# Score matmuls in turn on two row halves, and a decay broadcast in one matmul, in a two-layer encoder

## The chip, the cores and the metric

The kernel runs on one core of a Trainium2 chip, with all inputs in device memory. The metric is device time in microseconds, lower is better. A core has five engines that run their own instruction streams and meet at semaphores: TensorE (PE; its weight loads are listed apart as PEld), VectorE (DVE), ScalarE (ACT), GpSimd (POOL) and SyncE (SP), which here issues the weight transfers. PE multiplies a stationary operand by a moving one and writes to PSUM, eight banks of 512 float32 values for each of 128 partitions. A matmul whose operands lie on fewer than 128 partitions uses fewer rows of the array: operands on partitions 0 to 63 and on 64 to 127 use different row halves.

## The reference

Two residual layers over 256 tokens of width 2048, float32. The even layer mixes by gated linear attention (GLA) and two-dimensional neighbourhood attention, the odd one by a bidirectional Mamba-2 state-space mixer (SSD) and sliding-window attention; both end in an FFN of hidden width 5632. The two parts that the change touches:

```python
def gla_scan(q, k, v, log_a):            # 8 heads, dk = 64, per chunk
    ...
        b = jnp.cumsum(ai, axis=2)
        diff = b[:, :, :, None, :] - b[:, :, None, :, :]
        decay = jnp.exp(jnp.where(causal[:, :, None], diff, -jnp.inf))
        attn = jnp.einsum('bhtc,bhsc,bhtsc->bhts', qi, ki, decay)
    ...

def ssd_scan(xdt, da, bm, cm):           # 16 heads, both directions
    ...
    a_cum = jnp.cumsum(da.reshape(bn, n, l, g, j), axis=2)
    tri = jnp.tril(jnp.ones((l, l), dtype=bool))
    seg = a_cum[:, :, :, None] - a_cum[:, :, None]
    lmat = jnp.exp(jnp.where(tri[:, :, None, None], seg, -jnp.inf))
    cb = jnp.einsum('bnlgs,bnmgs->bnlmg', cc, bc)
    y_diag = jnp.einsum('bnlmg,bnmgj,bnmgjp->bnlgjp', cb, lmat, x)
    ...
```

GLA needs a score for each pair of tokens under a decay for each channel; SSD needs, for each head, the cumulated decay of every token against that of every other.

## The kernel before

**Weights.** All large products are float32 in three passes: a weight tile is loaded (`raw`), rounded to fp32r on ACT (`whi`, L184), and the rest is formed on DVE (`wlo`, L186); three matmuls add hi x hi, hi x lo and lo x hi. Projections with 512 moving columns are lines 211 to 213 (`acc`), those with 256 are 242 to 244 (`accb`). `whi` and `wlo` have seven buffers each, and the casts run ahead of PE until no buffer is free.

**Mixers in the background.** The mixers are generators, moved on a step at a time (`tick`) while the projections are written into the program, so small work lies between projection matmuls. The final order on each engine is set by the tile scheduler from priorities and a modelled timeline; it is fixed in the program.

**GLA scores.** The heads lie in pairs, 64 channels each, on the two row halves. For each of seven levels, and once more for the diagonal, `gla_attn` (L825) forms scaled q and k in `ge` and calls `gla_scores` (L811): for row half 0, then for row half 1, it takes a PSUM tile `gs` of 128x512 and writes four 128x128 matmuls with 64 rows (L821) into it. A float32 matmul stands in the trace as two matmul records with their weight loads. DVE then merges the tile into `gat` under a mask (L851, L857; for the first level ACT copies, L849). The scores across the two halves of the tokens (`gc`, L877) are made in the same way and copied by ACT (L878). There are two such generators, one for each half of the heads.

**SSD decay.** `ssd_dt` (L1104) makes the step sizes and their cumulated decay `ack` on 48 partitions: heads of the forward direction on rows 0 to 15, of the backward one on rows 32 to 47. It splits `ack` into fp32r parts side by side in `achl` (L1142 on ACT, L1143 on DVE), turns `ack` and the steps round with four small PE transposes (`dtT`, L1147 and L1148), and makes a selector `sel`, an identity of 48x48 (L1152). For each of 16 heads `ssd` (L1173) broadcasts the head's row to all partitions: for each direction a matmul of the selector's column with the high part and one with the low part, 48 rows and 256 columns, added up in the PSUM tile `acb` (L1199, L1200). DVE subtracts and cuts (L1204), ACT takes the exponential (L1206), DVE and POOL multiply, and PE uses the result (`yp`, L1226).

**Shared buffers.** All small PSUM tiles (`gs`, `acb`, `yp`, transposes and others) come from one pool of four banks, the projections' sums from another of four. `mtmp` tiles come in turn from six scratch buffers (512 float32 values for each partition), `slot` tiles from 26 larger ones.

Of the kernel before, what the change touches and what calls it, by code (L numbers as in the profile page):

```python
# [18 lines left out]
F32 = mybir.dt.float32  # L19
F32R = mybir.dt.float32r  # L20
# [6 lines left out]
P = 128  # L27
D = 2048
T = 256
# [62 lines left out]
class Trunk:  # L92
# [717 lines left out]

    def gla_scores(self, e):  # L811

        nc = self.nc
        res = []
        for i in range(2):
            ps = self.mx([P, 2, 2, P], "gs")
            r = slice(64 * i, 64 * i + 64)
            for tt in range(2):
                for j in range(2):
                    c = j * T + tt * P  # L820
                    nc.tensor.matmul(ps[:, tt, j], e[r, 1, c:c + P], e[r, 0, c:c + P], start=True, stop=True)  # L821
            res.append(ps)
        return res

    def gla_attn(self, half, qk, b):  # L825

        nc = self.nc
        qkf = qk.rearrange("p a j t -> p a (j t)")
        at = self.slot([P, 2, 4, P], nm="gat")
        for li, h in enumerate(LVLS):  # L830
            n = 512 // (2 * h)
            e = self.slot([P, 2, 512], nm="ge")
            f = b[:, 0].rearrange("p (n o h) -> p n o h", n=n, o=2)
            w = b[:, 1].rearrange("p (n o h) -> p n o h", n=n, o=2)
            eq = e[:, 0].rearrange("p (n o h) -> p n o h", n=n, o=2)
            ek = e[:, 1].rearrange("p (n o h) -> p n o h", n=n, o=2)
            fr = f[:, :, 0, h - 1:h].broadcast_to([P, n, h])
            wr = w[:, :, 1, 0:1].broadcast_to([P, n, h])
            nc.vector.tensor_sub(eq[:, :, 1], f[:, :, 1], fr)
            nc.vector.tensor_sub(eq[:, :, 0], w[:, :, 0], wr)  # L840
            nc.vector.tensor_sub(ek[:, :, 0], fr, f[:, :, 0])
            nc.vector.tensor_sub(ek[:, :, 1], wr, w[:, :, 1])
            nc.scalar.activation(e, e, AF.Exp, scale=1.0 / 16.0)
            yield
            nc.vector.tensor_mul(e, e, qkf)
            for i, ps in enumerate(self.gla_scores(e)):
                pv = ps.rearrange("p a b t -> p (a b) t")
                if li == 0:
                    nc.scalar.copy(at[:, i], pv)  # L849
                else:  # L850
                    nc.vector.copy_predicated(at[:, i], self.lv[:, li].unsqueeze(1).broadcast_to([P, 4, P]), pv)  # L851
            yield
        e = self.slot([P, 2, 512], nm="ge")
        nc.scalar.mul(e[:, 0], qkf[:, 0], 2.0)
        nc.scalar.copy(e[:, 1], qkf[:, 1])
        for i, ps in enumerate(self.gla_scores(e)):
            nc.vector.copy_predicated(at[:, i], self.lv[:, len(LVLS)].unsqueeze(1).broadcast_to([P, 4, P]),  # L857
                                      ps.rearrange("p a b t -> p (a b) t"))
        yield

        e = self.slot([P, 2, 2, 2, P], nm="gc")
        bv = b.rearrange("p d (j a t) -> p d j a t", j=2, a=2)
        nc.vector.tensor_copy(e[:, 0, :, 1], bv[:, 0, :, 1])
        nc.vector.tensor_copy(e[:, 0, :, 0], bv[:, 1, :, 0])
        nc.vector.tensor_sub(e[:, 1, :, 0], bv[:, 0, :, 0, P - 1:P].broadcast_to([P, 2, P]), bv[:, 0, :, 0])
        nc.vector.tensor_sub(e[:, 1, :, 1], bv[:, 1, :, 1, 0:1].broadcast_to([P, 2, P]), bv[:, 1, :, 1])
        ef = e.rearrange("p a j b t -> p a (j b t)")
        nc.scalar.activation(ef, ef, AF.Exp, scale=1.0 / 16.0)
        yield
        nc.vector.tensor_mul(ef, ef, qkf)  # L870
        cr = self.slot([P, 2, 4, P], nm="gcr")
        for i in range(2):
            ps = self.mx([P, 4, P], "gs")
            r = slice(64 * i, 64 * i + 64)
            for tt in range(2):
                for j in range(2):
                    nc.tensor.matmul(ps[:, 2 * tt + j], e[r, 1, j, 1 - tt], e[r, 0, j, tt], start=True, stop=True)  # L877
            nc.scalar.copy(cr[:, i], ps)  # L878
        yield
        return at, cr  # L880

# [221 lines left out]

    def ssd_dt(self, ps, row):  # L1104

        nc = self.nc
        R = 48

        def tl(nm):
            return self.mtmp([R, 2, T], nm=nm)  # L1110
        xu = tl("dx")
        x, u = xu[:, 0], xu[:, 1]
        nc.vector.tensor_mul(x, ps[0:R], row[0:R])
        nc.scalar.activation(u, x, AF.Abs, bias=self.dtb[0:R])
        dt = self.keep.tile([R, T], F32, tag="lrT", bufs=1, name="dtk")
        nc.vector.tensor_scalar(out=dt, in0=x, scalar1=self.dtb[0:R], scalar2=0.0, op0=ALU.add, op1=ALU.max)
        nc.scalar.activation(u, u, AF.Exp, scale=-1.0)
        ss2 = tl("ds")
        s, s2 = ss2[:, 0], ss2[:, 1]
        nc.vector.tensor_scalar_add(s, u, 2.0)  # L1120
        nc.vector.reciprocal(s, s)
        yield
        nc.vector.tensor_mul(s, s, u)
        nc.vector.tensor_mul(s2, s, s)
        q = x
        nc.vector.tensor_scalar_mul(q, s2, 1.0 / 15.0)
        for k in (13, 11, 9, 7, 5, 3):
            nc.vector.scalar_tensor_tensor(out=q, in0=q, scalar=1.0 / k, in1=s2, op0=ALU.add, op1=ALU.mult)
        yield
        nc.vector.scalar_tensor_tensor(out=q, in0=q, scalar=1.0, in1=s, op0=ALU.add, op1=ALU.mult)  # L1130
        nc.vector.scalar_tensor_tensor(out=dt, in0=q, scalar=2.0, in1=dt, op0=ALU.mult, op1=ALU.add)
        ea = self.small([R, 1], "ea")
        nc.scalar.activation(ea, self.alog[0:R], AF.Exp)
        da = u
        nc.vector.tensor_scalar(out=da, in0=dt, scalar1=ea, scalar2=-1.0, op0=ALU.mult, op1=ALU.mult)
        ac = self.slot([R, T], nm="ack")
        one = self.ones
        nc.vector.tensor_tensor_scan(ac[0:32], one[0:32], da[0:32], 0.0, ALU.mult, ALU.add)
        nc.vector.tensor_tensor_scan(ac[32:48][:, ::-1], one[32:48], da[32:48][:, ::-1], 0.0, ALU.mult, ALU.add)
        yield  # L1140
        hl = self.slot([R, 2, T], F32R, nm="achl")
        nc.scalar.copy(hl[:, 0], ac)  # L1142
        nc.vector.tensor_sub(hl[:, 1], ac, hl[:, 0].bitcast(F32))  # L1143
        tp = self.mx([P, 4, R], "dtT")
        for t in range(2):
            sl = slice(t * P, (t + 1) * P)
            nc.tensor.transpose(tp[:, t], ac[:, sl], self.ident[0:R, 0:R])  # L1147
            nc.tensor.transpose(tp[:, 2 + t], dt[:, sl], self.ident[0:R, 0:R])  # L1148
        nat = self.slot([P, 4, R], nm="dtn")
        nc.vector.tensor_copy(nat, tp)  # L1150
        sel = self.keep.tile([R, R], F32R, tag="sel", bufs=1, name="sel")
        nc.scalar.copy(sel, self.ident[0:R, 0:R])  # L1152
        self.have["dt"] = (hl, nat, sel)
        yield

# [17 lines left out]
    def ssd(self, g, bc, ssp):  # L1173

        nc = self.nc
        yield from self.need("dt", f"bc{g}0", f"bc{g}1")
        hl, nat, sel = self.have["dt"]
# [7 lines left out]
        for qd in range(2):  # L1185
# [8 lines left out]
            for hq in range(4):  # L1194
                h, hc = 8 * g + 4 * qd + hq, (4 * qd + hq) * 64
                pb = self.mx([P, 2, T], "acb")
                for d in range(2):
                    pick = sel[:, 32 * d + h:32 * d + h + 1].to_broadcast([48, P])
                    nc.tensor.matmul(pb[:, d], pick, hl[:, 0], start=True, stop=False)  # L1199
                    nc.tensor.matmul(pb[:, d], pick, hl[:, 1], start=False, stop=True)  # L1200
                s = self.slot([P, 6 * P], nm="seg")
                for c0, c1, d, l0, mt in parts:
                    r = 32 * d + h
# [4 lines left out]
                for i, (c0, c1, d, l0, mt) in enumerate(parts):  # L1208
                    r = 32 * d + h
                    if i in PSTT:  # L1210
                        nc.gpsimd.tensor_scalar(out=s[:, c0:c1], in0=s[:, c0:c1], scalar1=nat[:, 2 + mt, r:r + 1],
                                                scalar2=None, op0=ALU.mult)
                        if i == PSTT[-1]:
                            e = slice(parts[PSTT[0]][0], c1)
# [177 lines left out]
```

## Time and profile before

| | before |
|---|---|
| median of 3 runs | 2235.45 us (2234.25 to 2236.69) |
| the profiled execution | 2236.18 us |
| its span, first to last instruction | 2234.4 us |
| mean granted PE clock | 0.992 |
| `gs` matmul records | 288, from 76.2 to 194.0 us |
| `acb` matmul records | 64, from 1240.4 to 1404.0 us |

A profile row names a line (L821), an engine, an operation and tiles as output<-inputs. For PE, 64*128 are the rows and columns of the array in use, and 64x128 is the moving operand. A row of the timeline begins with its start and its duration in us. Matmul records overlap, so that the time a matmul takes from PE is read from one start to the next. A row of waits says who waited for whom, the total in us, how often, and the longest.

### The profile page before, as it was taken

The numbers are of one execution on the slowest core, as the hardware profiler recorded it, in microseconds if no ns is written. First come the engines' busy times: TensorE is split into PE (matmuls) and PEld (weight loads), VectorE is DVE, ScalarE is ACT, GpSimd is POOL, SyncE is SP. The second block draws the span as 40 slices with busy tenths as digits, with TensorE's granted clock in tenths as the row PEclk, the third lists the DMA queues.
The fourth block names the chain that finished last, engine by engine and source line by source line (L and its number), as shares of the span: only waits on it lengthen the run. The fifth ranks groups of instructions, "written<-read, shape, count | busy, mean of one in ns | idle before, by whom it ended". The sixth has DMA issues, their size and how long they took to land.

```text
span 2234.4 us, 29039 instructions
## 1 busy us (share of the span) xinstructions
PE 2189.1 (98%) x10888; PEld 1843.0 (82%) x10888; DVE 1773.0 (79%) x2134; ACT 1212.1 (54%) x1511; POOL 201.3 (9%) x246
## 2 busy tenths in 40 slices
PE   8999999999999999999989999999999999999997
PEld 7989998788888888888769988877888888888875
DVE  7877545766878888888989987766687889888896
ACT  6545345554555555555656545655556555555563
POOL 0001010210000000000021253121000000000002
PEclk9999999999999999999999999999999999999998
DMA  7445556575575655565656433657466565546563
GB/s 280 133 132 167 188 183 193 185 244 167 202 243 173 211 173 199 169 217 198 210 183 217 158 121 124 218 189 264 152 205 235 181 212 176 201 161 209 198 213 117
DMA packets 117325, 424.54 MB, mean 190 GB/s; under 512 B 13392, under 2 KB 13520, under 8 KB 117184
## 3 DMA queue, kind: packets, MB, share of 16 engines
q1 hardware_dynamic: 110592, 400.61, 53.4%
q0 software_dynamic: 6448, 21.99, 3.0%
q8 instruction: 85, 1.39, 0.2%
q14 instruction: 56, 0.46, 0.1%
q10 hardware_dynamic: 144, 0.10, 0.0%
HBM read 414.25 MB, written 8.39 MB: 189 GB/s over the span
## 4 chain that ended last, share of the span: by engine, by line
PE 88%; DVE 9%; issue 2%; DMA 1%; ACT 0%; POOL 0%; DVEq 0%; SPq 0%; ACTq 0%; POOLq 0%
PE acc L213 19%; PE acc L211 19%; PE acc L212 19%; PE sq L618 5%; PE sq L619 5%; PE sq L620 5%; DVE wlo L186 4%; PE accb L242 3%; PE accb L244 3%; PE accb L243 3%; DVE sw L567 1%; PE tp L285 1%; PE gs L821 1%; DVE f L627 1%; PE as L946 1%
## 5 line engine op out<-in xcount | busy, mean ns | idle before, releaser
L186 DVE TENSOR_TENSOR wlo<-raw,whi 128x1024 fp32r<-128x1024 f32 x596 | 741.7, 1252 | 292.4 <-ACT whi L184 284.5
L184 ACT CAST whi<-raw 128x1024 fp32r<-128x1024 f32 x596 | 624.5, 1051 | 580.6 <-PE acc L213 387.7
L213 PE MATMUL acc<-whi,xtl 128*128 128x512 f32 x1760 | 691.8, 394 | 6.0 <-DVE xtl L331 5.9
L212 PE MATMUL acc<-wlo,xth 128*128 128x512 f32 x1760 | 689.8, 393 | 0.6 <-DVE wlo L186 0.6
L211 PE MATMUL acc<-whi,xth 128*128 128x512 f32 x1760 | 677.3, 394 | 3.6 <-ACT xth L328 3.5
L184 ACT CAST whi<-sw 128x1024 fp32r<-128x1024 f32 x280 | 293.3, 1053 | 231.4 <-PE acc L213 132.6
L213 PEld LDWEIGHTS acc<-whi,xtl 128*128 128x128 f32 x1760 | 332.7, 189 | 77.6 <-DVE xtl L331 8.7
L211 PEld LDWEIGHTS acc<-whi,xth 128*128 128x128 f32 x1760 | 332.6, 189 | 73.9 <-ACT xth L328 5.4
L212 PEld LDWEIGHTS acc<-wlo,xth 128*128 128x128 f32 x1760 | 332.8, 189 | 70.8 <-DVE wlo L186 1.7
L186 DVE TENSOR_TENSOR wlo<-sw,whi 128x1024 fp32r<-128x1024 f32 x280 | 337.8, 1220 | 47.7 <-ACT whi L184 44.9
L619 PE MATMUL sq<-wlo,so 128*128 128x512 f32 x560 | 220.0, 393 | 4.5 <-DVE wlo L186 4.5
L620 PE MATMUL sq<-whi,so 128*128 128x512 f32 x560 | 219.2, 391 | 0.0
L618 PE MATMUL sq<-whi,so 128*128 128x512 f32 x560 | 219.2, 394 | 0.0
L567 DVE TENSOR_TENSOR sw<-sw,sw 128x1024 f32<-128x1024 f32 x160 | 193.8, 1220 | 17.9 <-DMA sw<-sstream 17.4
L242 PE MATMUL accb<-xth,whi 128*128 128x256 f32 x608 | 173.8, 286 | 0.0
L244 PE MATMUL accb<-xth,wlo 128*128 128x256 f32 x608 | 173.0, 285 | 0.0
L243 PE MATMUL accb<-xtl,whi 128*128 128x256 f32 x608 | 172.8, 284 | 0.0
L619 PEld LDWEIGHTS sq<-wlo,so 128*128 128x128 f32 x560 | 106.0, 189 | 28.6 <-DVE wlo L186 7.0
L620 PEld LDWEIGHTS sq<-whi,so 128*128 128x128 f32 x560 | 106.0, 189 | 22.5 <-DVE so L536 0.6
L618 PEld LDWEIGHTS sq<-whi,so 128*128 128x128 f32 x560 | 106.0, 189 | 22.2 <-ACT whi L184 0.4
L635 POOL DMA_DIRECT2D x<-xm x8 | 4.3, 544 | 1291.9 <-ACT whi L184 645.5
L242 PEld LDWEIGHTS accb<-xth,whi 128*128 128x128 f32 x608 | 116.5, 192 | 1.6 <-issue 0.7
(245 smaller groups left out, 2254.2 us busy)
## 6 DMA issues: line engine op xcount, KB each, us to landing
raw<-wstream SPq DMA_DIRECT2D x596, 512.0 KB, 4.9
sw<-sstream SPq DMA_DIRECT2D x160, 512.0 KB, 6.3
gb<-norm_gains POOLq DMA_DIRECT2D x16, 256.0 KB, 7.8
xm<-x POOLq DMA_DIRECT2D x16, 256.0 KB, 3.4
x<-xm POOLq DMA_DIRECT2D x8, 512.0 KB, 5.4
x<-x SPq DMA_DIRECT2D x4, 512.0 KB, 8.9
x<-x POOLq DMA_DIRECT2D x4, 512.0 KB, 7.7
xf<-x POOLq DMA_DIRECT2D x8, 256.0 KB, 3.2
```

Source lines behind the costliest of these rows:

```text
L184: self.pin(nc.scalar.copy(hi, src))
L186: self.pin(nc.vector.tensor_sub(lo, src, hi.bitcast(F32)))
L211: self.pin(nc.tensor.matmul(ps[t], xh, wh[:, k % 2], start=s, stop=False))
L212: self.pin(nc.tensor.matmul(ps[t], xh, wl[:, k % 2], start=False, stop=False))
L213: self.pin(nc.tensor.matmul(ps[t], xl, wh[:, k % 2], start=False, stop=e))
L242: nc.tensor.matmul(ps, wh[:, kt % 8], xh, start=kt == 0, stop=False)
L243: nc.tensor.matmul(ps, wh[:, kt % 8], xl, start=False, stop=False)
L244: nc.tensor.matmul(ps, wl[:, kt % 8], xh, start=False, stop=kt == 15)
L567: nc.vector.tensor_add(a, a, b)
L618: nc.tensor.matmul(ps, xh, wh[:, k], start=s, stop=False)
L619: nc.tensor.matmul(ps, xh, wl[:, k], start=False, stop=False)
L620: nc.tensor.matmul(ps, xl, wh[:, k], start=False, stop=e)
```

## The change

In `gla_scores`, and in `gla_attn` for the tile across halves, both PSUM tiles are taken first, and the matmuls of the two row halves are written in turn. A helper, `turn`, ties each matmul to the one before it in order on the engine, with no semaphore.

In `ssd_dt` the two parts are stacked: the high part on rows 0 to 15 and the low part on rows 32 to 47 of a tile of 128 rows, with the two directions side by side in its 512 columns and zeros in all other rows. The selector becomes 128x16, with the identity on both sets of rows. For this there are a memset and a full copy of zeros, and casts and a subtraction for each direction. In `ssd` one matmul of 128 rows and 512 columns for each head takes the place of four.

```diff
     def gla_scores(self, e):
-        for i in range(2):
-            ps = self.mx([P, 2, 2, P], "gs")
-            r = slice(64 * i, 64 * i + 64)
-            for tt in range(2):
-                for j in range(2):
-                    c = j * T + tt * P
-                    nc.tensor.matmul(ps[:, tt, j], e[r, 1, c:c + P], e[r, 0, c:c + P], start=True, stop=True)
-            res.append(ps)
+        res = [self.mx([P, 2, 2, P], "gs") for _ in range(2)]
+        for tt in range(2):
+            for j in range(2):
+                c = j * T + tt * P
+                for i in range(2):
+                    r = slice(64 * i, 64 * i + 64)
+                    self.turn(self.nc.tensor.matmul(res[i][:, tt, j], e[r, 1, c:c + P], e[r, 0, c:c + P],
+                                                    start=True, stop=True), i or tt or j)
         return res
+
+    def turn(self, ins, after):
+        if after:
+            self.tc.add_manual_dep(ins.ins, self.prev, mybir.DependencyInfo(
+                mybir.DependencyClass.NoSync, mybir.DependencyReason.DATA), reason="turn")
+        self.prev = ins.ins.name
...
     def ssd_dt(self, ps, row):
-        hl = self.slot([R, 2, T], F32R, nm="achl")
-        nc.scalar.copy(hl[:, 0], ac)
-        nc.vector.tensor_sub(hl[:, 1], ac, hl[:, 0].bitcast(F32))
+        hl = self.slot([P, 2, T], F32R, nm="achl")
+        zero = self.mtmp([P, 2, T], nm="dz")
+        nc.vector.memset(zero, 0.0)
+        nc.scalar.copy(hl, zero)
+        for d in range(2):
+            a = ac[32 * d:32 * d + 16]
+            nc.scalar.copy(hl[0:16, d], a)
+            hb = zero[32 * d:32 * d + 16, 0]
+            if d:
+                nc.vector.tensor_copy(hb, hl[0:16, d].bitcast(F32))
+            else:
+                hb = hl[0:16, d].bitcast(F32)
+            nc.vector.tensor_sub(hl[32:48, d], a, hb)
...
-        sel = self.keep.tile([R, R], F32R, tag="sel", bufs=1, name="sel")
-        nc.scalar.copy(sel, self.ident[0:R, 0:R])
+        sel = self.keep.tile([P, 16], F32R, tag="sel", bufs=1, name="sel")
+        nc.scalar.copy(sel, zero[:, 1, 0:16])
+        for d in range(2):
+            r = slice(32 * d, 32 * d + 16)
+            nc.scalar.copy(sel[r], self.ident[r, r])
...
     def ssd(self, g, bc, ssp):
-                for d in range(2):
-                    pick = sel[:, 32 * d + h:32 * d + h + 1].to_broadcast([48, P])
-                    nc.tensor.matmul(pb[:, d], pick, hl[:, 0], start=True, stop=False)
-                    nc.tensor.matmul(pb[:, d], pick, hl[:, 1], start=False, stop=True)
+                nc.tensor.matmul(pb.rearrange("p a t -> p (a t)"), sel[:, h:h + 1].to_broadcast([P, P]),
+                                 hl.rearrange("p a t -> p (a t)"), start=True, stop=True)
```

More of the change, by code (lines that the diff above doesn't have):

```diff
@@ L811, in gla_scores @@
     def gla_scores(self, e):
-        nc = self.nc
-        res = []
-        for i in range(2):
-            ps = self.mx([P, 2, 2, P], "gs")
-            r = slice(64 * i, 64 * i + 64)
-            for tt in range(2):
-                for j in range(2):
-                    c = j * T + tt * P
-                    nc.tensor.matmul(ps[:, tt, j], e[r, 1, c:c + P], e[r, 0, c:c + P], start=True, stop=True)
-            res.append(ps)
-        return res
+        res = [self.mx([P, 2, 2, P], "gs") for _ in range(2)]
[6 more added lines that the diff above has]
+                                                    start=True, stop=True), i or tt or j)
+        return res
+    def turn(self, ins, after):
[3 more added lines that the diff above has]
+        self.prev = ins.ins.name
     def gla_attn(self, half, qk, b):
@@ L871, in gla_attn @@
         cr = self.slot([P, 2, 4, P], nm="gcr")
-        for i in range(2):
[L873 to L878, printed above, removed]
+        res = [self.mx([P, 4, P], "gs") for _ in range(2)]
+        for tt in range(2):
+            for j in range(2):
+                for i in range(2):
+                    r = slice(64 * i, 64 * i + 64)
+                    self.turn(nc.tensor.matmul(res[i][:, 2 * tt + j], e[r, 1, j, 1 - tt], e[r, 0, j, tt],
+                                               start=True, stop=True), i or tt or j)
+        for i in range(2):
+            nc.scalar.copy(cr[:, i], res[i])
         yield
```

## The prediction

> **What bounds the kernel now.** I read the page's busy times first, then its chain of work that ended last, then the busy time in the two stretches where the changed lines run, then the list of waits there, and last the timeline of TensorE (PE) around single groups.
>
> ```profile
> PE 2189.1 (98%) x10888; PEld 1843.0 (82%) x10888; DVE 1773.0 (79%) x2134; ACT 1212.1 (54%) x1511; POOL 201.3 (9%) x246
> PE 88%; DVE 9%; issue 2%; DMA 1%; ACT 0%; POOL 0%; DVEq 0%; SPq 0%; ACTq 0%; POOLq 0%
> 70.00:200.00 130.00, 130.00 (x866) 113.22 (x865) 107.35 (x165) 63.84 (x75) 6.13 (x2) 1.00 0.45 146
> 1180.00:1420.00 240.00, 239.32 (x1467) 211.45 (x1466) 201.39 (x385) 131.99 (x218) 75.74 (x104) 1.00 0.48 154
> 1220.00:1230.00 10.00, 10.00 (x86) 9.81 (x85) 9.95 (x20) 5.12 (x8) 0.26 (x4) 1.00 0.50 163
> PEld gs L821 <- issue: 2.8, 8, 0.4
> ACT whi L184 <- PE accb L243: 24.0, 18, 2.3
> ```
>
> Rows three to five are stretches: length, then busy time of PE, PEld, DVE, ACT and POOL, then granted clock, DMA share and GB/s. In the stretch with the GLA scores (70 to 200 us) PE is busy for all of 130.00 us, in the SSD stretch (1180 to 1420) for 239.32 of 240.00, both at granted clock 1.00. DVE follows with 107.35 and 201.39, so it has 23 and 39 us to spare as a mean, though not everywhere: 9.95 of 10.00 us from 1220 to 1230. The last two rows are waits: the score matmuls wait for nothing but their own issue, and in the SSD stretch ScalarE's weight casts wait 18 times for PE to give a buffer back. Weight preparation is ahead of PE, so time taken off PE here should come off the end. What has to be priced is PE time from start to start, since matmuls overlap and their busy times add up to too much.
>
> **The change in the GLA scores.** Nothing is removed. The same 16 records per call (8 score matmuls, 2 records each) are put in another order: row half 0, row half 1, and so on, instead of eight and then eight. The rows of two stretches, PE only, and of the whole tile:
>
> ```profile
> 100.06 0.39 PE L213 MATMUL acc<-whi,xtl 128*128 128x512 f32 x1
> 100.29 0.39 PE L211 MATMUL acc<-whi,xth 128*128 128x512 f32 x1
> 100.60 1.71 PE L821 MATMUL gs<-ge 64*128 64x128 f32 x16
> 102.24 0.50 PE L212 MATMUL acc<-wlo,xth 128*128 128x512 f32 x1
> 102.58 0.39 PE L213 MATMUL acc<-whi,xtl 128*128 128x512 f32 x1
> ...
> 106.34 2.82 PE L821 MATMUL gs<-ge 64*128 64x128 f32 x32
> 109.08 0.50 PE L211 MATMUL acc<-whi,xth 128*128 128x512 f32 x1
> ...
> 180.15 1.16 PE L821 MATMUL gs<-ge 64*128 64x128 f32 x8
> 181.23 0.50 PE L211 MATMUL acc<-whi,xth 128*128 128x512 f32 x1
> ...
> L821 PE MATMUL gs<-ge x256: 272/272/373, 76.2 to 189.3; 64*128 64x128 f32 x128
> L877 PE MATMUL gs<-gc x32: 272/272/373, 146.9 to 194.0; 64*128 64x128 f32 x32
> ...
> 90.20:90.30 0.10, 0.10 (x3) 1.00 0.11 41
> 90.83:90.95 0.12, 0.12 (x7) 1.00 0.00 0
> ```
>
> 288 records are 18 sets of 16. A full set holds PE from 100.60 to 102.24, 1.64 us. Half a set alone, eight records on one row half, holds it from 180.15 to 181.23, 1.08 us. So two halves cost less than twice one half already: 1.64 against 2.16. The last two rows, stretches of another set, count the records in flight: three early on, seven where the first half ends and the second begins. Three is one chain (272 ns each), seven is two chains at once. So the two row halves do run side by side today, but only where the second half's records come up while the first half's last ones are still going. Interleaved from the first record, both chains can run for their whole length, and a set costs one chain, 1.08 us, plus a few ns: 0.55 us less.
>
> How many: following L821 and L877 along PE from 76.2 to 194.0 us there are seven single sets, five pairs of sets back to back (x32, such as 106.34 to 109.08, 2.74 us) and two lone halves of one set (x8). Single sets: 7 x 0.55 = 3.9 us. Pairs: in the lone half the eighth record starts at 180.15 + 1.16 - 0.27 = 181.04, so the seven steps take 0.89 us, 0.13 each, and the exit 0.19; sixteen in a chain take 1.08 + 8 x 0.13 = 2.12, 0.62 less than 2.74; five make 3.1. The lone halves join: one of two 1.08 goes, 1.1 us. Sum 8.1 us. Bounds: nothing at all, if interleaved issue is not served better than today's order; and 18 x 0.19 = 3.4 us more, if the exits were saved too. I take 8.1, since the seven in flight show two chains at full pace.
>
> What else the reorder does: both score tiles are taken from the four shared PSUM buffers before the first matmul, and the first is complete 0.2 us later than today (1.08 against 0.9). Its readers on DVE and ACT come later by that much, with DVE idle for 23 us of this stretch; cost nothing. Queued behind the score matmuls on PE are the projection matmuls; if a PSUM buffer is not free they all wait (priced among the rivals).
>
> **The change in the SSD decay broadcast.** Per head, four matmuls of 48 rows and 256 columns become one of 128 rows and 512 columns.
>
> ```profile
> 1259.96 0.28 PE L244 MATMUL accb<-xth,wlo 128*128 128x256 f32 x1
> 1260.17 0.38 PE L1199 MATMUL acb<-achl,sel 48*128 48x256 f32 x1
> 1260.39 0.28 PE L1200 MATMUL acb<-achl,sel 48*128 48x256 f32 x1
> ...
> 1260.63 0.28 PE L1200 MATMUL acb<-achl,sel 48*128 48x256 f32 x1
> 1260.84 0.39 PE L242 MATMUL accb<-xth,whi 128*128 128x256 f32 x1
> 1261.06 0.28 PE L243 MATMUL accb<-xtl,whi 128*128 128x256 f32 x1
> 1261.18 0.28 PE L244 MATMUL accb<-xth,wlo 128*128 128x256 f32 x1
> ...
> 1295.28 0.38 PE L1199 MATMUL acb<-achl,sel 48*128 48x256 f32 x1
> ...
> 1296.74 0.40 PE L212 MATMUL acc<-wlo,xth 128*128 128x512 f32 x1
> ...
> 1403.10 0.48 PE L213 MATMUL acc<-whi,xtl 128*128 128x512 f32 x1
> 1404.50 0.39 PE L212 MATMUL acc<-wlo,xth 128*128 128x512 f32 x1
> ```
>
> A 128x256 matmul normally follows another after 0.12 us (1261.06 to 1261.18), a 128x512 one after 0.23 (100.06 to 100.29). Around the four 48-row ones there is more: 0.21 into the first, 0.22 to the second, 0.21 out of the last, and 0.22 where 0.12 is normal after the first full-row matmul behind them. So from 1259.96 to 1261.06 one head costs 1.10 us; with one full-row 512-column matmul it is 0.12 + 0.23 + 0.12 = 0.47, 0.63 less. In the company of 512-column matmuls (1403.10 to 1404.50) it is 1.40 against 3 x 0.23 = 0.70, 0.70 less. Two heads back to back (1295.28 to 1296.74) are 1.46 against 3 x 0.23, 0.77 less, 0.38 a head. Eleven heads of the sixteen stand alone, four in two pairs, one is broken in two by other work: 11 x 0.63 + 4 x 0.38 + 1 x 0.8 = 9.3 us. About 0.1 us of each comes from the change of row count, not from the matmuls themselves; without it the floor is 16 x (4 x 0.12 - 0.23) = 4.0 us. Top: 16 x 0.70 = 11.2. I take 9.3, since in all three surroundings the delays stand in the rows.
>
> **What the SSD part adds,** once, around 1225 us. Nearest rows:
>
> ```profile
> L1142 ACT CAST achl<-ack x1: 406/406/406, 1225.5 to 1225.5; 48x256 fp32r<-48x256 f32 x1
> L1143 DVE TENSOR_TENSOR achl<-ack,achl x1: 409/409/409, 1227.5 to 1227.5; 48x256 fp32r<-48x256 f32 x1
> L684 DVE MEMSET ones<- x1: 272/272/272, 0.9 to 0.9; 128x256 f32 x1
> L878 ACT COPY gcr<-gs x4: 572/586/587, 148.1 to 194.4; 128x512 f32<-128x512 f32 x4
> L1199 PE MATMUL acb<-achl,sel x32: 272/279/382, 1240.4 to 1403.8; 48*128 48x256 f32 x32
> ```
>
> DVE: a 128x512 memset (twice 0.27), one more subtraction and one copy of 16x256 (at most 0.41 each), 1.4 us more. ACT: a 128x512 copy (0.59), one more 16x256 cast (0.41), and three small casts for the selector in place of one that today runs in the first microseconds (at most 0.41 each), 2.2 us more. No DMA is added. They lengthen the path to the first broadcast by some 3 us; it starts at 1240.4 and the last of its inputs is written at 1227.5 + 0.4, so 12 us of cover. DVE has none to spare at that place (9.95 of 10), but what hides 1.4 us there is the store of prepared weights, as the waits of the casts for PE show. If that cover is gone, PE waits those 1.4 us. The zero tile takes one of six shared scratch buffers; the convolutions that come after it wait for older ones, covered in the same way. Cost zero, bound 0 to 1.4 us.
>
> **Sum.** 8.1 + 9.3 = 17.4 us. The profiled execution took 2236.18 us (span 2234.4), which gives 2218.8; the median of the three runs is 0.73 lower, 2235.45, which gives 2218.0. A measurement of this kernel can tell about 0.2%, 4.5 us, from no change.
>
> [...]
>
> **The rivals.** The first rests on the smallest matmuls of the kernel:
>
> ```profile
> 1228.07 0.22 PE L1148 MATMUL dtT<-ca,dtk 48*128 48x48 f32 x1
> ...
> 1228.20 0.22 PE L1148 MATMUL dtT<-ca,dtk 48*128 48x48 f32 x1
> ```
>
> - Issue is the limit of the score sets. Even matmuls of 48 columns follow each other no faster than every 0.065 us (1228.07 to 1228.20 for two steps). A set is then 16 x 0.065 + 0.19 = 1.23 us, 0.15 more than forecast, and the gain is 18 x 0.15 = 2.7 us smaller: 2220.7. For: sixteen starts in 0.89 us are one every 0.056. Against: while a set waits to enter, its first records can queue up. Chance 0.13.
> - The turns change nothing, because PE looks far enough ahead by itself and the overlap of today is all there is: only the SSD part pays, 2235.5 - 9.3 = 2226.2. For: some overlap is there already. Against: seven in flight occur only in the middle of a set. Chance 0.10.
> - DVE, at 9.95 of 10 us before the broadcasts, becomes the bound of the SSD stretch and weights arrive late: what PE saves there is given back, 2235.5 - 8.1 = 2227.4. Against: 39 us of DVE idle over that stretch, and the casts wait for PE, not PE for them. Chance 0.10.
> - Slower: the score sets wait for PSUM. Both tiles are wanted at once and quicker sets want them sooner. If each set had to wait for two evacuations of 0.73 us, 18 x 1.45 = 26.1 us are lost: 2244.1. It ends slower by more than the bound of measurement from (17.4 + 4.5) / 18 = 1.22 us a set. The evacuation's row:
>
> ```profile
> L851 DVE COPY_PREDICATED gat<-lv,gs x24: 711/728/739, 94.6 to 189.3; 128x512 f32<-128x512 uint8 x24
> ```
>
>  Against: pairs of sets hold all four buffers today without a wait on PE but issue. Chance 0.04.
>
> **How the numbers follow.** The forecast has 0.60, on its own 2214 to 2222; the three smaller gains 0.13, 0.10, 0.10; slower 0.04; 0.03 is left for an order of instructions that comes out otherwise and eats most of it. The low end takes the upper bounds of both parts (3.4 and 1.9 us more): 2213. The high end takes in the cases at 2226 to 2227 with the 1.4 us of DVE: 2229. Faster by over 0.2% means under 2231: the first four cases less a little for two of them together, 0.88; the same 0.07; slower 0.05.
>
> **What would show it.** In the trace after: x16 score groups that hold PE for 1.1 us instead of 1.64, x32 ones for about 2.1 instead of 2.74, with seven or so in flight from the start; 16 broadcasts of 128x512 that cost 0.23 us with no 0.1 us steps around them; PE still busy for the whole of both stretches; everything after the mixers as before. Wrong would be: score records that start one after another 0.11 us apart; PE waits in front of gs, or whi and wlo waits of PE in the SSD stretch.

## The result, and the profile after

| | before | after |
|---|---|---|
| median of 5 runs | 2235.52 us (2234.25 to 2236.69) | 2222.42 us (2221.77 to 2224.21) |
| ratio, 95% interval | | 0.9941 [0.9930, 0.9952] |
| the profiled execution, its span | 2236.18, 2234.4 us | 2221.77, 2220.0 us |

The change made the kernel 13.1 us, 0.59%, faster. The forecast was 2218.0, and 4.3 us of the 17.4 did not come. The rows of the profile after, in the order of those of before: busy times, the chain that ended last, and the two stretches with the changed lines (length, then busy time of PE, PEld, DVE, ACT and POOL, granted clock, DMA share, GB/s):

```profile
PE 2173.3 (98%) x10840; PEld 1829.0 (82%) x10840; DVE 1772.4 (80%) x2137; ACT 1213.5 (55%) x1515; POOL 205.3 (9%) x246
PE 86%; DVE 10%; issue 2%; POOL 1%; DMA 1%; ACT 0%; DVEq 0%; POOLq 0%; ACTq 0%
70.00:200.00 130.00, 130.00 (x917) 112.15 (x916) 109.36 (x170) 64.53 (x77) 6.24 (x3) 1.00 0.46 154
1230.00:1410.00 180.00, 177.70 (x1027) 155.90 (x1026) 152.94 (x304) 99.99 (x172) 72.33 (x86) 1.00 0.43 141
```

PE is still the bound. In the GLA stretch it is busy for every one of 130.00 us. In the SSD stretch it now idles for 2.3 us of 180, where before the same row reads 180.00 of 180.00, and POOL, which had 0% of the chain, has 1%. Both are read further down.

**The GLA sets.** PE's timeline around a single set and around a pair, and the records in flight early in that first set:

```profile
88.33 1.16 PE L819 MATMUL gs<-ge 64*128 64x128 f32 x16
89.43 0.39 PE L243 MATMUL accb<-xtl,whi 128*128 128x256 f32 x1
...
103.62 2.06 PE L819 MATMUL gs<-ge 64*128 64x128 f32 x32
105.61 0.50 PE L211 MATMUL acc<-whi,xth 128*128 128x512 f32 x1
...
88.83:88.95 0.12, 0.12 (x6) 0.12 (x6) 0.00 (x0) 0.00 (x0) 1.00 1.51 375
```

A whole set holds PE for 88.33 to 89.43, 1.10 us, where it held it for 1.64; a pair 1.99 us instead of 2.74. Six records are in flight half a microsecond into the set, and its first two start 6 ns apart (worked out from the records), so both chains run from the start. But five of the eighteen sets look like this:

```profile
98.02 0.48 PE L819 MATMUL gs<-ge 64*128 64x128 f32 x2
98.43 0.50 PE L213 MATMUL acc<-whi,xtl 128*128 128x512 f32 x1
...
99.55 1.16 PE L819 MATMUL gs<-ge 64*128 64x128 f32 x14
100.64 0.50 PE L211 MATMUL acc<-whi,xth 128*128 128x512 f32 x1
...
96.47 1.35 DVE L856 COPY_PREDICATED gat<-lv,gs 128x512 f32<-128x512 uint8 x2
```

The set is cut after its first matmul (two records). Four projection matmuls lie between it and the other seven, in the program's order and not by a wait on the chip: the last row, DVE's timeline, shows the merges of the previous set, which give the PSUM buffers back one after the other, and done at 97.82. The reading is that in the schedule the first matmul went as soon as one buffer was free, and the second, which writes to the other tile, a merge later; the run with both tiles held, below, bears it out. A cut costs a second entry and exit of the row halves: 98.02 to 98.43 is 0.41 us, while the 14 records after it take 1.09, as much as 16.

**The SSD broadcast.** PE's timeline at two heads, one among 256-column and one among 512-column matmuls:

```profile
1251.73 0.28 PE L244 MATMUL accb<-xth,wlo 128*128 128x256 f32 x1
1251.85 0.40 PE L1218 MATMUL acb<-achl,sel 128*128 128x512 f32 x1
1252.09 0.28 PE L242 MATMUL accb<-xth,whi 128*128 128x256 f32 x1
1252.21 0.28 PE L243 MATMUL accb<-xtl,whi 128*128 128x256 f32 x1
...
1315.69 0.39 PE L213 MATMUL acc<-whi,xtl 128*128 128x512 f32 x1
1315.91 0.39 PE L1218 MATMUL acb<-achl,sel 128*128 128x512 f32 x1
1316.14 0.40 PE L211 MATMUL acc<-whi,xth 128*128 128x512 f32 x1
```

The broadcast enters after 0.12 us, takes 0.24 and leaves the next step at 0.12: 1251.73 to 1252.21 is 0.48 us, against 1.10 before. Among 512-column matmuls it is one more of 0.23. What took the rest is in the waits of PE over this stage (total, times, longest) and in the timelines behind them, PE, POOL and DVE:

```profile
PE yp L1245 <- POOL seg L1239: 2.3, 2, 1.5
...
1305.96 1.10 PE L1245 MATMUL yp<-xs,seg 128*128 128x64 f32 x8 [1.47 <-POOL seg L1239]
1307.89 1.10 PE L1245 MATMUL yp<-xs,seg 128*128 128x64 f32 x8 [0.83 <-POOL seg L1239]
...
1295.66 4.39 POOL L1230 TENSOR_SCALAR seg<-seg,dtn 128x128 f32<-128x128 f32 x2 [8.59 <-ACT seg L1225]
1300.13 0.95 POOL L1234 TENSOR_TENSOR seg<-seg,cbx 128x256 f32<-128x256 f32 x1
1301.07 3.92 POOL L1230 TENSOR_SCALAR seg<-seg,dtn 128x128 f32<-128x128 f32 x2
1304.96 0.95 POOL L1239 TENSOR_TENSOR seg<-seg 128x256 f32<-128x256 f32 x1
...
L1230 POOL TENSOR_SCALAR seg<-seg,dtn x32: 600/892/2222, 1240.8 to 1398.1; 128x128 f32<-128x128 f32 x32
...
1295.88 1.23 DVE L186 TENSOR_TENSOR wlo<-raw,whi 128x1024 fp32r<-128x1024 f32 x1
1297.01 0.91 DVE L1236 SCALAR_TENSOR_TENSOR seg<-seg,dtn,cbx 128x256 f32<-128x256 f32 x2
1297.85 0.68 DVE L999 TENSOR_TENSOR rq<-rq,cc 128x512 f32<-128x512 f32 x1
1298.45 1.21 DVE L186 TENSOR_TENSOR wlo<-raw,whi 128x1024 fp32r<-128x1024 f32 x1
```

PE comes to a head's products (`yp`) sooner, and POOL's sum for their factor (L1239) is not there yet. Two products of 128x128 by a scalar took POOL 4.39 us, the next two 3.92, about 2 us each, where the fastest of the 32 took 0.60. Meanwhile DVE ran one TENSOR_TENSOR or SCALAR_TENSOR_TENSOR after another (the last rows, 1295.88 to 1299.66). The stretching itself is not new: before, the slowest of these products took 2.31 us, but PE waited for none of them:

```profile
L1211 POOL TENSOR_SCALAR seg<-seg,dtn x32: 597/872/2311, 1245.5 to 1410.7; 128x128 f32<-128x128 f32 x32
```

**Where the time came from.** The sum of PE's steps between the same two projection matmuls, worked out from the records, is free of what happens elsewhere in the run. For the GLA stage (between the matmuls that start at 65.1 and 240.1 us in the trace of before) it is 175.01 us before and 168.94 after, 6.1 less (forecast 8.1); for the SSD stage (1220.1 and 1490.1) 270.06 and 263.58, 6.5 less (forecast 9.3). Outside the two stages, loading and normalising move by up to 2.6 us from run to run, also in a kernel with neither part of the change.

### The profile page after: what moved, and what is told of

Same layout as the page of the kernel before. It is cut to its first block, busy times and chain, and to the rows that moved or that the text cites. A ratio compares the mean times of both kernels' runs of the same rounds, so it can differ in the third digit from the quotient of the medians.

```text
span 2220.0 us, 28963 instructions
## 1 busy us (share of the span) xinstructions
PE 2173.3 (98%) x10840; PEld 1829.0 (82%) x10840; DVE 1772.4 (80%) x2137; ACT 1213.5 (55%) x1515; POOL 205.3 (9%) x246
## 4 chain that ended last, share of the span: by engine, by line
PE 86%; DVE 10%; issue 2%; POOL 1%; DMA 1%; ACT 0%; DVEq 0%; POOLq 0%; ACTq 0%
PE acc L213 19%; PE acc L212 19%; PE acc L211 19%; DVE wlo L186 5%; PE sq L618 5%; PE sq L619 5%; PE sq L620 5%; PE accb L242 3%; PE accb L244 3%; PE accb L243 3%; PE tp L285 1%; DVE sw L567 1%; DVE xtl L331 1%; DVE f L627 1%; PE gs L819 1%
```

## The experiments

The medians of each kernel are of five to eleven runs, beside runs of the kernel before on the same chip. Two versions 1 us apart cannot be told apart by medians (a half interval is 2 to 3 us); there the stage sums decide, of one trace for each kernel. GLA and SSD in this table are the changes of those sums against before.

| kernel | median | before | ratio, 95% interval | GLA | SSD |
|---|---|---|---|---|---|
| after | 2222.42 | 2235.52 | 0.9941 [0.9930, 0.9952] | -6.07 | -6.48 |
| GLA part alone | 2227.88 | 2235.51 | 0.9966 [0.9953, 0.9978] | -6.07 | -0.02 |
| SSD part alone | 2230.30 | 2235.51 | 0.9976 [0.9967, 0.9985] | +0.03 | -4.81 |
| tiles held | 2221.56 | 2235.51 | 0.9939 [0.9926, 0.9951] | -7.78 | -6.45 |
| `yp` a step later | 2228.14 | 2235.51 | 0.9966 [0.9952, 0.9979] | -6.07 | -2.27 |
| products on ACT | 2221.31 | 2235.93 | 0.9935 [0.9921, 0.9949] | -6.04 | -8.56 |
| tiles held, products on ACT | 2218.39 | 2235.93 | 0.9924 [0.9911, 0.9936] | -7.79 | -8.56 |
| before, products on ACT | 2236.28 | 2235.93 | 1.0003 [0.9994, 1.0011] | 0.00 | +0.27 |
| broadcast on 48 rows | 2230.03 | 2235.93 | 0.9973 [0.9963, 0.9982] | -6.05 | +2.13 |
| turns of two matmuls | 2224.57 | 2235.41 | 0.9952 [0.9938, 0.9965] | -4.83 | -4.81 |

**Each part alone.** One kernel keeps `ssd_dt` and `ssd` of before, the other `gla_scores` and `gla_attn` of before.

> The GLA turns alone, SSD as before. Theory A (the turns work as priced, but five of the eighteen sets are cut open after their first matmul, 0.6 us each): the stage gains what it gained in the trace of the changed kernel, 6.1 us, so 2229.4 us, with five lone x2 groups of gs. Rival B (the gain in that stage belongs to another order of everything, not to the turns): anything but 6 us, and sets not shorter. If both parts add up, this run and the one with SSD alone have gains that sum to 13.1.

> The one-matmul broadcast alone, GLA as before. Theory A (16 broadcasts gain 8 to 9 us of PE time, and PE gives back what it then waits for POOL's seg in front of yp): 2235.5 - 8.5 = 2227.0 if the two waits of 2.6 us do not come here, 2229.5 if they do. Rival B (the broadcast gains only its matmul count, 4.0 us): 2231.5.

The GLA part gains 7.6 us by the medians, the SSD part 5.2; the sum, 12.8, is the whole change's 13.1 within the noise. So the parts do not hinder each other, and each falls short by itself in its stage. The SSD part alone has the same wait on PE, to the tenth. Behind it stands something more, shown by a stretch (columns as in the rows above) and PE's timeline in it:

```profile
PE yp L1238 <- POOL seg L1232: 2.3, 2, 1.5
...
1316.52:1319.93 3.41, 3.41 (x11) 2.73 (x10) 2.49 (x8) 0.84 (x1) 0.13 (x1) 0.50 0.00 0
...
1318.05 0.63 PE L213 MATMUL acc<-whi,xtl 128*128 128x512 f32 x1
1318.48 0.63 PE L211 MATMUL acc<-whi,xth 128*128 128x512 f32 x1
```

Right after the two waits the granted clock was 0.50 for 3.41 us, and projection matmuls followed each other every 0.43 us instead of 0.23. By these two steps, 3.41 us x (1 - 0.23 / 0.43), that costs this trace an estimated 1.6 us, nearly all of its distance to the whole change in the SSD stage (4.8 against 6.5). In the trace of the whole change the same two waits left the clock at 1.00.

**Both tiles held before the set starts.** A one-column memset by DVE on both tiles makes the schedule wait for both buffers before the first matmul. The memsets take tile 0, then tile 1, and the turns begin with half 1:

```diff
         res = [self.mx([P, 2, 2, P], "gs") for _ in range(2)]
+        self.hold([t[:, 0, 0, 0:1] for t in res])
...
-                for i in range(2):
+                for i in (1, 0):
```

> The changed kernel, with one column of both score tiles set by DVE ahead of a set, so that both PSUM buffers are held before its first matmul and no set is cut open. Theory A (a cut set pays one entry and one exit of the row half more, about 0.6 us): five cuts less, 3.0 us, 2219.4, and no x2 group of gs. Rival B (the projection matmuls that slip into a cut have to run anyway, a cut costs nothing): 2222.4. Rival C (36 small DVE instructions and later sets cost more than that): above 2222.4.

PE's timeline at the set that was cut above, and the one wait of PE from 60 to 240 us, where before and after have none:

```profile
102.18 1.16 PE L820 MATMUL gs<-ge 64*128 64x128 f32 x16
103.27 0.50 PE L212 MATMUL acc<-wlo,xth 128*128 128x512 f32 x1
...
PE go L906 <- ACT gcr L892: 0.7, 1, 0.7
```

No set is cut any more, and the GLA stage gains 7.8 us instead of 6.1, so keeping the sets whole is worth 1.7 us, 0.34 for each cut, with the new wait of 0.7 us on the other side; 0.6 each was expected. The median moved by 0.9 us only, which is within its spread. The cut is shown as the cause of the missing GLA gain by the stage sum, not by the median.

**`yp` one step later.** If PE only comes too early, more background work ahead of it should help: one more `yield` ahead of `yp`.

> The changed kernel, with one more step of the mixers' background between the products of a head and its yp matmuls, so that yp is put later in PE's order. Theory A (PE stood 1.6 and 1.0 us in front of yp because POOL was late): both waits go, 2222.4 - 2.6 = 2219.8. Rival B (the wait is POOL's throughput, and moves to a later yp): 2222.4. Rival C (later yp holds buffers longer and costs elsewhere): above.

The early waits went, but it is 5.7 us slower than after. PE's waits at the mixers' end:

```profile
PE apt L976 <- DVE sc L969: 1.8, 1, 1.8
PE apo L986 <- DVE smv L965: 1.7, 1, 1.7
...
PEld yp L1246 <- POOL seg L1239: 0.3, 1, 0.3
```

The whole chain of the SSD heads slid back, and at about 1395 us the mixers' tail ran out of projection matmuls to hide behind. A delay was the wrong repair; it shows that the stage has little slack at its end.

**POOL's products on ACT.**

```diff
-                        nc.gpsimd.tensor_scalar(out=s[:, c0:c1], in0=s[:, c0:c1], scalar1=nat[:, 2 + mt, r:r + 1],
-                                                scalar2=None, op0=ALU.mult)
+                        nc.scalar.mul(s[:, c0:c1], s[:, c0:c1], nat[:, 2 + mt, r:r + 1])
```

> The changed kernel, with the 32 products of 128x128 by the step sizes (two for each head) on ACT instead of POOL. Theory A (PE stood 2.6 us in front of yp because four of these products took 1.9 to 2.2 us each on POOL, instead of 0.8, while DVE ran subtractions and products with two SBUF inputs): no wait of PE for seg, 2222.4 - 2.6 = 2219.8, and the products 0.3 to 0.4 us each on ACT. Rival B (it is the order that is late, the next link, POOL's product with cbx, then makes PE wait): 2222.4. Rival C (ACT is late with the weights' casts for the 12 us more): above.

> The kernel before, with the same products on ACT. A control: before, PE did not stand in front of yp, so theory A expects no gain, 2235.5 (2234 to 2237). If it gains 2 us or more, moving the products is a gain of its own, and the gain of the run above on it does not belong to the lost wait.

The products' row, in the change with this edit:

```profile
L1230 ACT ACTIVATE seg<-seg,dtn x32: 384/392/457, 1241.9 to 1401.6; 128x128 f32<-128x128 f32 x32
```

On ACT all 32 take 0.38 to 0.46 us each. No `yp` waits, and the SSD stage gains 8.6 us instead of 6.5; the median, 1.1 us lower than that of the change, could not show it. The control says why this is not simply a better kernel: the same edit on the kernel before gains nothing (1.0003 [0.9994, 1.0011]). POOL's slow products cost time only once PE had become quicker.

**Both repairs.**

> Both repairs on the changed kernel: score sets held whole, and the products on ACT. Theory A (two separate losses): the gains of the two add up. The trace of the held run gained 1.7 us more in the GLA stage than the changed kernel; with 2.6 for the SSD stage that gives 2222.4 - 4.3 = 2218.1. Rival: no better than the better of the two alone.

PE's busy time over both stretches, and the only wait of PE that is left from 1230 to 1410 us:

```profile
70.00:200.00 130.00, 129.26 (x931) 112.80 (x930) 109.50 (x196) 66.45 (x77) 6.36 (x2) 1.00 0.48 160
1230.00:1410.00 180.00, 179.56 (x1034) 157.57 (x1033) 153.06 (x302) 109.17 (x203) 43.23 (x54) 1.00 0.44 144
...
PE apo L993 <- ACT pT L989: 0.4, 1, 0.4
```

2218.39 us (2218.04 to 2219.37), 17.5 us less than before, with the two stages at 7.8 and 8.6. In the GLA stretch PE idles only for the 0.7 us seen with the tiles held. With both leaks closed the forecast's 8.1 and 9.3 are there, less 1.0. This version beats both kernels; the intervals of its ratio and of the change's still overlap by a little, but no run of the one reaches a run of the other (its highest is 2219.37, the lowest of the change 2221.77).

**The broadcast on 48 rows.** One 512-column matmul as in the change, but of 48 rows, to price the change of row count by itself:

```diff
-                nc.tensor.matmul(pb.rearrange("p a t -> p (a t)"), sel[:, h:h + 1].to_broadcast([P, P]),
-                                 hl.rearrange("p a t -> p (a t)"), start=True, stop=True)
+                nc.tensor.matmul(pb.rearrange("p a t -> p (a t)"), sel[0:48, h:h + 1].to_broadcast([48, P]),
+                                 hl[0:48].rearrange("p a t -> p (a t)"), start=True, stop=True)
```

> The changed kernel, with the one matmul of the broadcast on 48 rows instead of 128 (the zero-filled rows are left out of the product). It takes the matmul count apart from the row count. Theory A (a change of the rows in use costs PE 0.1 us each at the entry, at the first matmul, at the exit and behind it): 16 heads x about 0.3 us in 15 places, 4.7 us slower, 2227; the 512-column matmul itself the same 0.23. Rival B (the gain was the matmul count alone): 2222.4.

```profile
1255.12 0.28 PE L244 MATMUL accb<-xth,wlo 128*128 128x256 f32 x1
1255.33 0.50 PE L1218 MATMUL acb<-achl,sel 48*128 48x512 f32 x1
1255.75 0.38 PE L242 MATMUL accb<-xth,whi 128*128 128x256 f32 x1
1255.97 0.28 PE L243 MATMUL accb<-xtl,whi 128*128 128x256 f32 x1
...
1312.80:1319.63 6.83, 6.81 (x19) 5.27 (x20) 3.96 (x12) 1.69 (x2) 1.71 (x3) 0.50 0.02 7
```

1255.12 to 1255.97 is 0.85 us against 0.48 with 128 rows: 0.21 into it, 0.42 to the next, and 0.22 where 0.12 is normal. That is 0.37 at each of 14 places (two heads stand together twice), some 5.2 us over the stage. The run is 7.6 us slower than after, and in the trace the stage is 8.6 us longer. The rest is the clock: the last row is a stretch right after the second wait for POOL, 6.83 us at a granted clock of 0.50, which by estimate costs up to half of that, 3.4 us. Of the 0.62 us that a head gained, from 1.10 to 0.48, 0.25 come from the smaller number of matmuls and 0.37 from the zero-filled rows.

**Turns of two matmuls.** The loop over `i` outside that over `j`: two matmuls (four records) of one row half, then two of the other.

> The changed kernel, but the row halves take turns every two score matmuls (four records) instead of every one. It asks how far ahead PE takes records for an idle row half. Before, with eight records a half, the second half began when the first was at its fifth record, so four lay between. Theory A (PE looks about four records ahead): the second half begins with the first, the two chains run side by side as with turns of one, a whole set still holds PE 1.1 us, and the GLA stage gains about 6 us. Rival B (only neighbours in the program run together): a set has overlap at its three borders only and holds PE about 1.4 us, the stage gains some 3 us. The sets are cut open in four places instead of five.

PE's timeline at the first set, and the records of `gs` in flight in its first 30 ns:

```profile
88.78 1.26 PE L819 MATMUL gs<-ge 64*128 64x128 f32 x16
89.97 0.39 PE L243 MATMUL accb<-xtl,whi 128*128 128x256 f32 x1
...
88.77:88.80 0.03, 0.02 (x2) 0.02 (x2) 0.00 (x0) 0.00 (x0) 1.00 0.66 273
```

Two records start within 30 ns. In the lone half of before (180.15 us), records of one half start 0.11 to 0.21 us apart (worked out from the records), so the second one is of the other half, and it starts although three more records of the first half stand ahead of it in the program. A set takes 1.19 us, 0.09 more than in single turns, 0.45 less than before. So turns need not be single ones, but single ones are best. The GLA stage gained 4.8 us with four of its sets cut, between the two theories. (Its SSD stage gained as little as that of the SSD part alone; here too the clock was 0.50 for 3.41 us after the waits.)

## Why the prediction was right, and where it was off

- *PE is the bound, and PE time from start to start is what counts*: right. The stage sums with both repairs, 7.8 + 8.6 = 16.4 us, agree with 17.5 of the medians to within what moves outside the stages.
- *A set costs one chain, 1.08 us*: right. 1.10 for a set, 1.99 for a pair (forecast 2.12).
- *Eighteen whole sets, and taking both PSUM tiles before the first matmul "cost nothing"*: this step failed. The prediction priced a PSUM buffer that comes late as a stall of PE, gave that 0.04, and found no such stall. It came in another form: the scheduler fixes the order with its own model of when a buffer comes free, and fills the gap with other matmuls. Five cuts of 0.34 us, 1.7 us in all, measured by taking them away.
- *A broadcast costs 0.23 us with no 0.1 us steps around it*: right, 0.24, and the 48-row run confirms that the steps come from the row count: 0.37 at each place.
- *The added work at the setup is hidden*: right. The last of the inputs:

```profile
L1161 DVE TENSOR_TENSOR achl<-ack,dz x1: 415/415/415, 1225.6 to 1225.6; 16x256 fp32r<-16x256 f32 x1
L1218 PE MATMUL acb<-achl,sel x16: 389/438/582, 1236.6 to 1391.1; 128*128 128x512 f32 x16
```

  It is written at 1226.0, 10.6 us ahead of the first broadcast.
- *What PE saves in the SSD stage comes off the end*: this step failed by 2.1 us, what the stage gained with the products on ACT. The prediction looked at DVE and ACT, found 39 us of DVE idle, and did not weigh POOL, the engine that finishes half of the factors for `yp`, and which was busy for 9% of the run. The products' longest, 2.31 us against 0.60, stood in the trace of before; there PE began the `yp` of the same two heads only 0.92 and 0.08 us after POOL's sum was done (worked out from the records), so the slack was almost used up. Its own sign, PE busy for the whole of both stretches, failed by these waits, 2.3 us of 180. The rival "DVE becomes the bound of the stage" had the right neighbour, but not the mechanism: DVE was not late itself; POOL was, while DVE was busy.
- *Rivals*: issue as the limit of the sets (1.23 us) fell, since 15 steps take 0.89 us, 0.059 each where the rival had 0.065; the pair's 32 records from 103.62 us start within 2.06 - 0.27 = 1.79 us, one every 0.058. "The turns change nothing" fell with the GLA part alone, at 7.6 us by the median and 6.1 in the stage.
- The range held the time, and what was missing lay within its two terms, 2.0 us of 8.1 and 2.8 of 9.3; the outcome came between the forecast and the rivals that lost one part whole. The prediction has no term for the half clock that three other kernels showed behind the same two waits; that the trace of the change was spared it is luck.

## What to carry to other kernels

When PE is the bound and is made quicker in a stage, look at each engine that feeds it there and at the longest instance of its operation and at how long before its use the result is there, not at its busy share or its median: what was ready 0.92 and 0.08 us ahead is a wait now. When two tiles are to be written in turn, make sure that the order of the program keeps the set whole; a helper write that claims both buffers first was worth 0.34 us for each cut here. A matmul of 48 rows among matmuls of 128 paid for the change of rows at both edges here, 0.37 us, and with zeros in the unused rows it took 0.24 us, like any other of 512 columns (0.23).

## What the hardware showed that was not expected

**POOL's products stretch beside DVE.** The six products of 128x128 that took POOL 0.60 to 0.61 us had a TENSOR_TENSOR or SCALAR_TENSOR_TENSOR of DVE beside them for 10 to 65% of that time; the ten that took 1.3 us or more had one for 72 to 100% (worked out from the records of the change; of the two runs the longest are 2.22 and 2.31 us). But twelve of the sixteen between, at 0.72 to 1.04 us, had one beside them all the time as well, so its presence alone does not set the duration. This is a correlation, and what stretches a product was not tested by itself; what was tested is that the same products on ACT, at 0.38 to 0.46 us, are not stretched.

**PE looks ahead across row halves.** In turns of four records the second half's first record starts within 30 ns of the first half's. The seven in flight of the kernel before have the same cause: in the set at 90 us the second half's first record started 0.55 us into the set, with three of the first half's eight still to start. So in both a record started past three that stood ahead of it. In the order of eight and eight a set still holds PE for 1.64 us, in turns of four records for 1.19. How far it can look at most was not measured.

**Half clock behind a short wait.** Of the five kernels with the waits for POOL, three had a stretch of 3.41 or 6.83 us at a granted clock of 0.50 at the second wait or just behind it (the SSD part alone, the broadcast on 48 rows, the turns of two matmuls). The change itself had none (its row from 1230 to 1410 us above stands at 1.00), nor had the run with tiles held, whose SSD stage gained as much (6.45 us against 6.48). Without these waits, the same stretch stands at 1.00 too, before and with both repairs. What decides whether it comes was not tested.
